# Silu in place, the weight sums of the last product one pair earlier, and other places for its first weights

## The chip, the cores and the metric

The kernel runs on one core of one Trainium2 chip. The metric is the device time of one execution in microseconds (us). A core has five engines that work side by side and wait for each other through semaphores: TensorE (PE, matrix products), VectorE (DVE), ScalarE (ACT), GpSimd (POOL) and SyncE (SP). Data moves between the main memory (DRAM) and the on-chip memory by DMA transfers; here SP, ACT and POOL issue them, each from its own queue of instructions, in order. An instruction whose condition is not met holds up all that stands behind it on the same engine.

## The reference

One layer of a hybrid encoder for 512 tokens of width 1024: four token mixers side by side, merged by gates; a cross-attention into 256 memory tokens; and a gated feed-forward part. The change lies in the feed-forward part alone:

```
hf = rms_norm(x, norm_ffn_pre)                     # 512 x 1024
u = dwconv_causal(hf @ w_up, ffn_dw) + ffn_dw_b    # 512 x 5632, three taps along the tokens
u_g, u_v = split(u, 2)                             # gate and value, 2816 columns each
yff = (silu(u_g) * u_v) @ w_down                   # 512 x 1024
x = x + rms_norm(yff, norm_ffn_post)
```

All of it is in float32.

## The kernel before

**Products.** A float32 operand is split into a high and a low part (ACT casts the high part, DVE subtracts it: tiles `wh` and `wl` for weights, `hth` and `htl` for activations), and each product is three matmuls: high by high, low by high, high by low. A matmul writes 512 columns of a bank of the accumulation memory (`ps_mm`, `ps_av`, `ps_sc`, `ps_tr`).

**The up product** has 22 blocks j of 128 columns, each with a gate half (i = 0) and a value half (i = 1). `done` takes a finished bank: ACT copies it into the tile `c` with bias and one tap, DVE adds the other two taps (L624), and behind the value half ACT computes Silu of the gate into a tile `th` of its own (L1681), and DVE multiplies it with the value into `qa` (L1683). There is one buffer for `th`. Nine of the blocks (j = 3, 5, ..., 19; the loop over q = 0 to 8) go through a scheme of seven products in place of eight, `seven(j)`. It loads the weights of the block into two tiles `wq`, forms sums of them on POOL, splits them in several steps, and its last split frees a tile `wq` for the next iteration. The block j + 1 follows in the plain way, mixed in.

**The last product** multiplies by `w_down`, 22 blocks of 128 rows taken as 11 pairs q = 0 to 10. It, too, goes by seven products in place of eight, so it needs sums of the four half blocks of a pair. The class `Sums` makes them during the up product. For each pair `load` brings two blocks of 512 KB into two tiles `wp` (L568, ACT's queue), `add` does four additions of 128x512 (L572 to L575), and `store` writes both tiles to a DRAM tensor `sums` (L579, ACT's queue). Pair 0 is added by DVE at the start of the loop; in iteration q, pair q + 1 is added by POOL; and pair 10 is loaded, added by DVE and stored behind the up product. The engine that adds matters for what stands behind it.

`down_jobs` then runs the last product in two phases over the pairs. In phase 0 a pair has two jobs of 12 matmuls each: job 0 needs half a block of `w_down` and one sum, job 1 two sums. SP loads the operands of a job into a tile `dw` (L591); ACT and DVE split it (L1652, L1653). POOL forms the sums on the side of the activations meanwhile (`pairs` and `qa`, L1664 to L1666 and L1870).

**Four places.** The tiles `wp`, `wq` and `dw` share four places of 512 KB, dw0 to dw3: `wp` takes turns in dw0 and dw1, `wq` in dw2 and dw3, and `dw` goes round all four. `dw_tile` keeps a counter for each name; without an entry the first tile goes to place 0:

```
i = ns.dw[name] = (ns.dw.get(name, -1) + 1) % n
return ns.fp.tile([P, D], dtype, tag=f"dw{first + i}", name=name)
```

A new tile in a place waits for the last user of the tile before.

**Order.** The order of the instructions on each engine is fixed when the kernel is built: a scheduler merges the jobs of the loops by its own estimates of time, and `issue_after` keeps a step behind a named instruction. Which of two steps stands first on an engine can therefore change with any edit.

Of the kernel before, what the change touches and what calls it, by code (L numbers as in the profile page):

```python
# [17 lines left out]
F32 = mybir.dt.float32  # L18
F32R = mybir.dt.float32r
AF = mybir.ActivationFunctionType  # L20
ALU = mybir.AluOpType
# [4 lines left out]
P = 128  # L26
S = 512
# [7 lines left out]
NF = DFF // P  # L35
# [51 lines left out]
def hybrid_layer(ctx: ExitStack, tc: tile.TileContext, a: dict, out: bass.AP):  # L87
    nc = tc.nc
    V, A, G, PE, SP = nc.vector, nc.scalar, nc.gpsimd, nc.tensor, nc.sync
# [1105 lines left out]
    ns = SimpleNamespace()  # L1195

    def then(f):

        return None, None, f
# [420 lines left out]
    def open_ffn():  # L1620
        bg.drain("n1")
        close(ns.work_)
        close(ns.xp_)
        close(ns.xm_)
        ns.fp_, ns.fp = new_pool("ffn", False)
        ns.work = ns.fp
        ns.quart = [ns.fp.tile([P, 4, S // 2], F32, tag=f"qa{q}", name="qa") for q in range(NF // 2)]
        ns.tok = [ns.fp.tile([P, 4, 4, S // 2], F32R, tag=n, name=n) for n in ("tokh", "tokl")]
        ns.post = ns.fp.tile([P, D], F32, name="g_ffn")
        ns.dw = {}  # L1630
        G.dma_start(ns.post, a["norm_ffn_post"][0].partition_broadcast(P))

    def dw_tile(name, n=4, first=0, dtype=F32):
# [34 lines left out]
    def up_jobs():  # L1668
        st, held = {}, []
        HALF = S // 2  # L1670
        first, second = slice(0, HALF), slice(HALF, S)

        def done(j, i, ps):
            if i == 0:
                st[j] = ns.fp.tile([P, 2, S], F32, tag="c", name="c", bufs=2)
            c, ch = st[j], i * NF + j
            st["first"] = A.activation(c[:, i], ps, AF.Identity, bias=pc("fb", ch), scale=pc("fdw2", ch)).ins
            st["taps"] = taps(c[:, i], ps, lambda k: pc("fdw01", k * 44 + ch), 3).ins
            if i == 1:
                th = ns.fp.tile([P, S], F32, tag="th", name="th")  # L1680
                A.activation(th, c[:, 0], AF.Silu)  # L1681
                x = ns.quart[j // 2][:, 2 * (j % 2):2 * (j % 2) + 2]
                V.tensor_tensor(x.rearrange("p a b -> p (a b)"), th, c[:, 1], ALU.mult)  # L1683

        def block(j, i):
            return cols(w_up, i * DFF + j * P)
# [1 line left out]
        def add_sums(q, eng, anchor):  # L1688
            with tc.issue_after(st[anchor]):
                ns.sums.add(q, eng)  # L1690

        def sums_step(what, q, anchor):
            if q < NF // 2:
                with tc.issue_after(st[anchor]):
                    getattr(ns.sums, what)(q)

        def plain(j, i, then=None):
            def body(hi, lo):
                ps = bank()
                channel_major(ps, (hi, lo), ns.hf)  # L1700
                done(j, i, ps)
                if then:
                    then()
            return *block(j, i), body
# [85 lines left out]
        for q, j in enumerate(range(3, NF - 2, 2)):  # L1790
            load_a, body_a, b, c, d, e = seven(j)
            if q:
                a = load_a, None, body_a
            else:
                a, early = (lambda: (ns,), None, lambda *w: body_first(*early)), []
                body_first = body_a
                yield then(lambda f=load_a: early.extend(f()))
                yield plain(2, 0)
                yield plain(2, 1, lambda: add_sums(0, V, "taps"))
            tail = {}  # L1800

            def first_half(hi, lo, tail=tail):
                tail.update(ps=bank(), w=(hi, lo))
                for k in range(4):
                    mm3(tail["ps"], hi[:, k], lo[:, k], ns.hf[0][:, k], ns.hf[1][:, k], k == 0, False)

            def second_half(j, tail=tail):
                hi, lo = tail["w"]
                for k in range(4, NK):
                    mm3(tail["ps"], hi[:, k], lo[:, k], ns.hf[0][:, k], ns.hf[1][:, k], False, k == NK - 1)  # L1810
                done(j, 1, tail["ps"])

            yield a
            yield plain(j + 1, 0)
            yield then(lambda q=q: sums_step("store", q, "first"))
            yield b
            yield (*block(j + 1, 1), first_half)
            yield then(lambda q=q: sums_step("load", q + 1, "taps"))
            if j + 4 > NF:
                ns.pair_sums = []  # L1820
                yield then(lambda: (down_places(("z7", 2)), down_sums(0, 1)))
            yield c
            yield d
            yield then(lambda j=j, f=second_half: f(j + 1))
            yield e
            yield then(lambda q=q: ns.sums.add(q + 1, G))
        q = NF // 2 - 1
        yield then(lambda: down_places(("tokh", 8), ("tokl", 1)))
        yield plain(NF - 1, 0, lambda: (sums_step("store", q - 1, "taps"), down_sums(2, 3)))
        yield plain(NF - 1, 1, lambda: (sums_step("load", q, "taps"), ns.sums.add(q), ns.sums.store(q),  # L1830
                                        down_sums(*range(4, NF // 2))))

    def down_jobs():
        pairs, hold, half = NF // 2, 4, S
# [229 lines left out]
```

## Time and profile before

| | |
|---|---|
| runs | 1078.36, 1080.32, 1084.20 us |
| median | 1080.32 us |
| profiled execution, its own time | 1078.18 us |
| its span | 1076.4 us (1.78 us lie around it) |
| mean granted TensorE clock | 0.987 |
| DMA moved | 169.42 MB, 157 GB/s |
| `wq` loads, `wp` loads, `wp` stores | 18, 22 and 22 of 512 KB |
| `dw` loads from `sums` | 44 of 256 KB |

The span is the stretch from the first to the last recorded instruction of the profiled execution, and all times of the trace count from its start. The mixers and the cross-attention take about the first 700 us, the up product runs to 936 us, the last product to about 1050 us, and the final normalisation to the end. Rows of the trace give the start, the length, the engine, the line of the kernel, and output and inputs; a bracket gives how long the engine had stood idle before, and what ended that. ACTq and SPq mark the instructions with which an engine issues a DMA. "x2" is two instructions in a row.

### The profile page before, as it was taken

How to read it: one execution, taken by the hardware profiler on the slowest of the kernel's cores; microseconds unless marked ns; L12 is line 12 of the kernel's file. 1: busy time of each engine (PE TensorE's matmuls, PEld its weight loads, DVE VectorE, ACT ScalarE, POOL GpSimd, SP SyncE). 2: the span in 40 equal slices, each digit the busy share in tenths (PEclk: the TensorE clock that was granted, in tenths of full speed). 3: DMA queues.
4: the chain of work that ended last, by engine and by line, in shares of the span. 5: the costliest groups of instructions: out<-in, count | busy, mean ns of one | idle time of the engine just before them, and what ended most of it. 6: DMA issues, size and time to landing. Idle time of an engine off the chain costs nothing.

```text
span 1076.4 us, 15302 instructions
## 1 busy us (share of the span) xinstructions
PE 1029.0 (96%) x5513; PEld 885.0 (82%) x5513; DVE 861.7 (80%) x1287; ACT 533.7 (50%) x898; POOL 317.3 (29%) x315
## 2 busy tenths in 40 slices
PE   9999999999999999999999999998999899767996
PEld 7888888888889888888888999996888888646885
DVE  7999998678787668878678987788776778876696
ACT  5322322386654566756345656545343553525662
POOL 3001000100111144232010421393665776891001
PEclk9999999999999999999999999999999999978999
DMA  8954333334534356766478332434566555446562
GB/s 272 302 156 103 98 98 98 93 89 119 151 111 126 87 145 190 192 179 178 147 226 270 131 119 78 124 112 156 176 197 201 191 181 172 156 157 235 183 211 85
DMA packets 194130, 169.42 MB, mean 157 GB/s; under 512 B 25295, under 2 KB 165692, under 8 KB 194053
## 3 DMA queue, kind: packets, MB, share of 16 engines
q1 hardware_dynamic: 185011, 136.69, 42.8%
q10 hardware_dynamic: 6482, 23.21, 5.8%
q0 software_dynamic: 2560, 8.54, 2.4%
q8 instruction: 43, 0.70, 0.3%
q14 instruction: 34, 0.28, 0.1%
HBM read 142.18 MB, written 26.23 MB: 156 GB/s over the span
## 4 chain that ended last, share of the span: by engine, by line
PE 70%; DVE 12%; DMA 8%; issue 4%; ACT 3%; POOL 2%; SPq 0%; ACTq 0%; DVEq 0%; POOLq 0%
PE ps_mm L244 33%; PE ps_av L244 18%; PE ps_tr L244 10%; PE ps_sc L244 6%; DVE wl L202 4%; DMA wq<-in_w_up 4%; DVE c L624 3%; DMA dw<-sums 2%; ACT wh L201 1%; PE ps_tr L250 1%; DVE qa L1683 1%; DMA ptl<-turned 1%; DMA turned<-e 1%; POOL pairs L1664 1%; DVE wl L1653 1%
## 5 line engine op out<-in xcount | busy, mean ns | idle before, releaser
L201 ACT CAST wh<-wr 128x1024 fp32r<-128x1024 f32 (+1 forms) x122 | 127.2, 1046 | 163.4 <-PE ps_mm L244 62.7
L202 DVE TENSOR_TENSOR wl<-wr,wh 128x1024 fp32r<-128x1024 f32 (+1 forms) x122 | 165.5, 1358 | 33.1 <-ACT wh L201 32.4
L244 PE MATMUL ps_mm<-hth,wl 128*128 128x512 f32 (+1 forms) x464 | 170.5, 376 | 1.2 <-DVE wl L202 1.2
L244 PE MATMUL ps_mm<-htl,wh 128*128 128x512 f32 (+1 forms) x464 | 170.5, 376 | 0.0
L244 PE MATMUL ps_mm<-hth,wh 128*128 128x512 f32 (+1 forms) x464 | 170.4, 376 | 0.0
L244 PEld LDWEIGHTS ps_mm<-hth,wl 128*128 128x128 f32 x464 | 85.5, 188 | 17.8 <-DVE wl L202 2.3
L244 PEld LDWEIGHTS ps_mm<-hth,wh 128*128 128x128 f32 x464 | 85.6, 188 | 14.8 <-ACT hth L164 0.3
L244 PEld LDWEIGHTS ps_mm<-htl,wh 128*128 128x128 f32 x464 | 85.5, 188 | 14.9
L244 PE MATMUL ps_av<-htl,wh 128*128 128x512 f32 (+1 forms) x256 | 94.6, 370 | 0.0
L244 PE MATMUL ps_av<-hth,wh 128*128 128x512 f32 (+1 forms) x256 | 94.6, 370 | 0.0
L244 PE MATMUL ps_av<-hth,wl 128*128 128x512 f32 (+1 forms) x256 | 94.5, 369 | 0.0
L697 DVE SCALAR_TENSOR_TENSOR y<-y,par,y 128x508 f32<-128x508 f32 (+29 forms) x120 | 83.1, 734 | 0.1
L1681 ACT ACTIVATE th<-c 128x512 f32<-128x512 f32 x22 | 13.9, 632 | 95.0 <-DVE qa L1683 57.0
L202 DVE TENSOR_TENSOR wl<-wq,wh 128x1024 fp32r<-128x1024 f32 (+1 forms) x27 | 37.4, 1385 | 26.2 <-ACT wh L201 26.2
L244 PEld LDWEIGHTS ps_av<-htl,wh 128*128 128x128 f32 x256 | 48.1, 188 | 8.0
L244 PEld LDWEIGHTS ps_av<-hth,wl 128*128 128x128 f32 x256 | 48.2, 188 | 7.8
L244 PEld LDWEIGHTS ps_av<-hth,wh 128*128 128x128 f32 x256 | 48.1, 188 | 7.5
L1653 DVE TENSOR_TENSOR wl<-dw,wh 128x1024 fp32r<-128x1024 f32 x32 | 42.5, 1330 | 13.4 <-ACT wh L1652 13.0
L244 PE MATMUL ps_tr<-hth,wh 128*128 128x512 f32 (+1 forms) x116 | 42.4, 366 | 8.7 <-ACT wh L201 8.7
L1652 ACT CAST wh<-dw 128x1024 fp32r<-128x1024 f32 x32 | 33.5, 1049 | 25.2 <-DMA dw<-sums 11.2
L244 PE MATMUL ps_tr<-hth,wl 128*128 128x512 f32 (+1 forms) x116 | 41.5, 358 | 0.9 <-DVE wl L202 0.9
L244 PE MATMUL ps_tr<-htl,wh 128*128 128x512 f32 (+1 forms) x116 | 41.7, 360 | 0.0
(556 smaller groups left out, 2826.2 us busy)
## 6 DMA issues: line engine op xcount, KB each, us to landing
wr<-in_w_in SPq DMA_DIRECT2D x38, 512.0 KB
wr<-in_w_gate SPq DMA_DIRECT2D x32, 512.0 KB
wr<-in_w_up SPq DMA_DIRECT2D x26, 512.0 KB
wp<-in_w_down ACTq DMA_DIRECT2D x22, 512.0 KB
sums<-wp ACTq DMA_DIRECT2D x22, 512.0 KB
dw<-sums SPq DMA_DIRECT2D x44, 256.0 KB
wq<-in_w_up SPq DMA_DIRECT2D x18, 512.0 KB
wr<-in_w_branch SPq DMA_DIRECT2D x16, 512.0 KB
```

The costliest lines, as they stand in the source:

```text
L201: last_weights[:] = [order(A.copy(hi, raw[:, :n])).ins, low.tensor_tensor(lo, raw[:, :n], hi.bitcast(F32), ALU.subtract).ins]
L202: low.tensor_tensor(lo, raw[:, :n], hi.bitcast(F32), ALU.subtract).ins]
L244: steps_of[:] = [PE.matmul(ps, lhs, rhs, start=start, stop=stop, skip_group_check=again).ins]
L250: turns.append(PE.transpose(ps, x, ident[:n, :n]).ins)
L624: ins = V.scalar_tensor_tensor(dst[:, s:], src[:, :S - s], w(k), dst[:, s:], ALU.mult, ALU.add)
L697: ins = V.scalar_tensor_tensor(dst[:, s:], src[:, :S - s], pc("conv_dw", k * 4 + j), dst[:, s:], ALU.mult, ALU.add)
L1652: A.copy(hi, x)
L1653: V.tensor_tensor(lo, x, hi.bitcast(F32), ALU.subtract)
L1664: G.tensor_tensor(t[:, 0], x[:, 1], x[:, 3], ALU.add)
L1681: A.activation(th, c[:, 0], AF.Silu)
L1683: V.tensor_tensor(x.rearrange("p a b -> p (a b)"), th, c[:, 1], ALU.mult)
```

## The change

Three things are changed. First, `ns.dw` starts with an entry: the first tile `dw` goes to place 2, so the last product begins in dw2 and dw3 and not in dw0 and dw1. Second, Silu writes over the gate half of `c`; the tile `th` is gone. Third, the sums go through the loop one pair earlier. Pair 0 is added and stored and pair 1 loaded ahead of the first iteration, DVE adds pair 1 in iteration 0, and in iteration q the pair q + 1 is stored, q + 2 loaded and, by POOL, added. Behind the loop only the store of pair 10 is left.

```diff
@@ open_ffn
-        ns.dw = {}
+        ns.dw = {"dw": 1}
@@ done, in up_jobs
             if i == 1:
-                th = ns.fp.tile([P, S], F32, tag="th", name="th")
-                A.activation(th, c[:, 0], AF.Silu)
+                A.activation(c[:, 0], c[:, 0], AF.Silu)
                 x = ns.quart[j // 2][:, 2 * (j % 2):2 * (j % 2) + 2]
-                V.tensor_tensor(x.rearrange("p a b -> p (a b)"), th, c[:, 1], ALU.mult)
+                V.tensor_tensor(x.rearrange("p a b -> p (a b)"), c[:, 0], c[:, 1], ALU.mult)
@@ ahead of the first iteration
-                yield plain(2, 0)
-                yield plain(2, 1, lambda: add_sums(0, V, "taps"))
+                yield plain(2, 0, lambda: (add_sums(0, V, "taps"), sums_step("store", 0, "taps")))
+                yield plain(2, 1, lambda: sums_step("load", 1, "taps"))
@@ the loop over q
-            yield then(lambda q=q: sums_step("store", q, "first"))
+            yield then(lambda q=q: (q or add_sums(1, V, "taps"), sums_step("store", q + 1, "first")) and None)
...
-            yield then(lambda q=q: sums_step("load", q + 1, "taps"))
+            yield then(lambda q=q: sums_step("load", q + 2, "taps"))
...
-            yield then(lambda q=q: ns.sums.add(q + 1, G))
-        q = NF // 2 - 1
+            yield then(lambda q=q: ns.sums.add(q + 2, G))
@@ behind the loop
-        yield plain(NF - 1, 0, lambda: (sums_step("store", q - 1, "taps"), down_sums(2, 3)))
-        yield plain(NF - 1, 1, lambda: (sums_step("load", q, "taps"), ns.sums.add(q), ns.sums.store(q),
-                                        down_sums(*range(4, NF // 2))))
+        yield plain(NF - 1, 0, lambda: (sums_step("store", NF // 2 - 1, "taps"), down_sums(2, 3)))
+        yield plain(NF - 1, 1, lambda: down_sums(*range(4, NF // 2)))
```

On SP, at the end of the up product, these loads begin the last product before the change. A number behind a name tells the tiles apart; dw_8922 is job 0 of pair 0, and dw_9000, dw_8928 and dw_9151 belong to the pairs 1 and 3, in dw2 and dw3.

```order
L591 DMA dw_9000<-sums_6869 128x512 [waits DMAHW4_49,DMAHW3_49,DVE_49]
L591 DMA dw_9000<-sums_6869 128x512 [waits DMAHW5_49,DMAHW4_49]
L591 DMA dw_8928<-in_w_down 128x512 [waits DMAHW7_49,DMAHW6_49,DVE_49]
L591 DMA dw_8928<-sums_6869 128x512 [waits DMAHW0_49]
L591 DMA dw_9151<-in_w_down 128x512 [waits DMAHW4_49,DMAHW7_49,DMAHW0_49,DVE_49]
L591 DMA dw_9151<-sums_6869 128x512 [waits DMAHW5_49]
L591 DMA dw_8922<-in_w_down 128x512 [waits DMASW5_49,DMAHW1_49,DMASW3_49,DMAHW3_49,PE_49,Pool_49]
L591 DMA dw_8922<-sums_6869 128x512
```

On SP at the same place after the change, dw_8916 and dw_8913 are the jobs 1 and 0 of pair 0, dw_9097 and dw_9039 those of pair 2, and dw_8919 and dw_8989 the jobs 0 and 1 of pair 1.

```order
L591 DMA dw_8916<-sums_6869 128x512 [waits DMAHW7_49,DMAHW3_49,DVE_49]
L591 DMA dw_8916<-sums_6869 128x512 [waits DMAHW0_49]
L591 DMA dw_8913<-in_w_down 128x512 [waits DMAHW3_49,DMAHW2_49,DVE_49]
L591 DMA dw_8913<-sums_6869 128x512 [waits DMAHW4_49]
L591 DMA dw_9097<-sums_6869 128x512 [waits DMAHW7_49,DMAHW0_49,DVE_49]
L591 DMA dw_9097<-sums_6869 128x512 [waits DMAHW1_49]
L591 DMA dw_9039<-in_w_down 128x512 [waits DMAHW3_49,DMAHW4_49,DMAHW2_49,DVE_49]
L591 DMA dw_9039<-sums_6869 128x512
L591 DMA dw_8919<-in_w_down 128x512 [waits DMASW5_49,DMAHW1_49,DMASW3_49,DMAHW5_49,PE_49,Pool_49]
L591 DMA dw_8919<-sums_6869 128x512 [waits DMAHW6_49]
L591 DMA dw_8989<-sums_6869 128x512 [waits DMAHW7_49,DMAHW4_49,PE_49]
L591 DMA dw_8989<-sums_6869 128x512 [waits DMAHW0_49]
```

The load that waits for POOL (the last addition of the pair that lies in dw0) is that of pair 0 before, and that of pair 1 now; both jobs of pair 0 and of pair 2 stand ahead of it.

On PE, the end of the 24 matmuls of pair 0 and the beginning of pair 1 after the change; `wr` and `hth` are split activations of pair 0 and pair 1, wh_8998 is the high part of dw_8916, wh_9042 that of dw_8919, wh_9105 that of dw_8989. Before, the first matmul behind the up product is the one on the high part of dw_8922.

```order
L244 MATMUL ps_av_9116<-wh_8998,wr_8922 128x512 [waits DVE_49,Activation_49]
L244 MATMUL ps_av_9116<-wl_8999,wr_8922 128x512
L244 MATMUL ps_av_9116<-wh_8998,wr_8923 128x512
L244 MATMUL ps_sc_9109<-wh_9042,hth_8992 128x512 [waits Activation_49]
L244 MATMUL ps_sc_9110<-wh_9042,hth_8992 128x512
L244 MATMUL ps_tr1_9111<-wh_9042,hth_8992 128x512
L244 MATMUL ps_tr0_9112<-wh_9042,hth_8992 128x512
L244 MATMUL ps_mm_9113<-wh_9105,hth_8992 128x512 [waits Activation_49]
L244 MATMUL ps_mm_9114<-wh_9105,hth_8992 128x512
L244 MATMUL ps_av_9115<-wh_9105,hth_8992 128x512
L244 MATMUL ps_av_9116<-wh_9105,hth_8992 128x512
L244 MATMUL ps_sc_9109<-wl_9043,hth_8992 128x512 [waits DVE_49]
```

Pair 0 stands in front of the wait for dw_8919, and pair 2 behind pair 1.

On DVE, ahead of the first iteration of the loop, before the change:

```order
L624 SCALAR_TENSOR_TENSOR c<-ps_av,par_398,c 128x511
L572 TENSOR_TENSOR wp<-wp 128x512
L202 TENSOR_TENSOR wl<-wq,wh 128x1024
L1653 TENSOR_TENSOR tokl<-qa,tokh 128x1024
L1683 TENSOR_TENSOR qa<-th,c 128x512
L573 TENSOR_TENSOR wp<-wp 128x512
L202 TENSOR_TENSOR wl<-wq,wh 128x512
L624 SCALAR_TENSOR_TENSOR c<-ps_mm,par_398,c 128x510
L574 TENSOR_TENSOR wp<-wp 128x512
L624 SCALAR_TENSOR_TENSOR c<-ps_mm,par_398,c 128x511
L575 TENSOR_TENSOR wp<-wp 128x512
L202 TENSOR_TENSOR wl<-wq,wh 128x1024
```

On DVE after the change, from the last tap that stands at the same place to the same split of `wq` at the end; the additions of pair 0 stand ahead of these rows.

```order
L624 SCALAR_TENSOR_TENSOR c<-ps_av,par_398,c 128x511
L1653 TENSOR_TENSOR tokl<-qa,tokh 128x1024
L1682 TENSOR_TENSOR qa<-c 128x512
L202 TENSOR_TENSOR wl<-wq,wh 128x512
L624 SCALAR_TENSOR_TENSOR c<-ps_mm,par_398,c 128x510
L624 SCALAR_TENSOR_TENSOR c<-ps_mm,par_398,c 128x511
L572 TENSOR_TENSOR wp<-wp 128x512
L573 TENSOR_TENSOR wp<-wp 128x512
L574 TENSOR_TENSOR wp<-wp 128x512
L575 TENSOR_TENSOR wp<-wp 128x512
L1774 TENSOR_TENSOR ps_tr_7103<-ps_tr_7103,mu 128x256
L202 TENSOR_TENSOR wl<-wq,wh 128x1024
```

The four additions here belong to pair 1, which has to be loaded first; the split of `wq` stands behind them. POOL's last addition of the pair in dw0 (L575) keeps its place behind 13 sums of activations; only the pair is another, 10 and not 9.

## The prediction

> **What bounds the kernel now.** I read the page first, for the engine that is busy most.
>
> ```profile
> PE 1029.0 (96%) x5513; PEld 885.0 (82%) x5513; DVE 861.7 (80%) x1287; ACT 533.7 (50%) x898; POOL 317.3 (29%) x315
> ```
>
> TensorE is busy for 96% of the span, so no edit can win more than TensorE's idle time and its slow clock. The windows view tells where those are. Its columns are the stretch and its length, the busy time and count of PE, PEld, DVE, ACT and POOL, the granted clock, the DMA share and GB/s.
>
> ```profile
> 930.00:940.00 10.00, 6.17 (x28) 4.77 (x26) 8.27 (x10) 4.35 (x7) 9.92 (x12) 0.99 0.29 105
> 940.00:950.00 10.00, 0.00 (x0) 0.00 (x0) 8.05 (x8) 3.73 (x8) 10.00 (x10) 0.50 0.24 72
> 950.00:960.00 10.00, 7.40 (x24) 5.96 (x25) 7.42 (x8) 4.01 (x5) 10.00 (x10) 0.66 0.66 214
> 960.00:970.00 10.00, 10.00 (x45) 8.20 (x44) 7.76 (x7) 2.32 (x3) 7.95 (x7) 1.00 0.45 162
> 970.00:980.00 10.00, 4.52 (x14) 3.29 (x13) 5.92 (x6) 4.59 (x7) 2.77 (x2) 0.70 0.87 302
> 980.00:1050.00 70.00, 70.00 (x309) 57.90 (x308) 55.64 (x61) 44.01 (x58) 2.56 (x4) 0.99 0.60 196
> 952.50:971.50 19.00, 18.70 (x72) 14.90 (x72) 14.29 (x13) 6.49 (x10) 15.45 (x14) 0.89 0.54 185
> ```
>
> PE does nothing for most of 936 to 952 and again around 971 to 977, and behind each pause the clock is down (0.66, 0.70). From 980 on it is full. The waits view, for the time behind 690 us, names what PE waited for (us in total, times, longest):
>
> ```profile
> PE ps_sc L244 <- ACT wh L1652: 21.9, 2, 16.4
> PE ps_tr L244 <- ACT wh L201: 8.7, 7, 1.6
> ```
>
> The first line is the two pauses, 16.4 and 5.5 us. The second is a short stall in seven of the nine iterations of the up product. The timeline of POOL, SP, ACT and PE gives the chain behind the first pause.
>
> ```profile
> 930.08 1.62 POOL L574 TENSOR_TENSOR wp<-wp 128x512 f32<-128x512 f32 x1
> 931.66 0.73 POOL L1664 TENSOR_TENSOR pairs<-qa 128x256 f32<-128x256 f32 x1
> ...
> 944.80 1.71 POOL L575 TENSOR_TENSOR wp<-wp 128x512 f32<-128x512 f32 x1
> 914.81 0.81 SPq L591 DMA_DIRECT2D dw<-sums  x2
> 919.50 0.33 SPq L591 DMA_DIRECT2D dw<-in_w_down  x1
> ...
> 946.54 0.33 SPq L591 DMA_DIRECT2D dw<-in_w_down  x1
> 946.92 4.78 SPq L591 DMA_DIRECT2D dw<-sums  x5
> 951.51 1.04 ACT L1652 CAST wh<-dw 128x1024 fp32r<-128x1024 f32 x1 [1.16 <-DMA dw<-sums]
> ...
> 955.01 1.04 ACT L1652 CAST wh<-dw 128x1024 fp32r<-128x1024 f32 x1 [1.94 <-DMA dw<-sums]
> 935.78 0.39 PE L244 MATMUL ps_av<-hth,wl 128*128 128x512 f32 x1
> 952.60 1.22 PE L244 MATMUL ps_sc<-wh,wr 128*128 128x512 f32 x2 [16.43 <-ACT wh L1652]
> ```
>
> POOL is through with three of four additions of pair 9 at 931.7, then does 13 sums of activations, and ends the fourth at 946.5. Only then may SP load pair 0 into dw0; ACT splits it at 951.5, and PE starts at 952.6. The pairs 1 and 3, in the other places, were loaded long before (914.8, 919.5). The second pause has the same form, with DVE in POOL's stead:
>
> ```profile
> 965.07 1.14 DVE L572 TENSOR_TENSOR wp<-wp 128x512 f32<-128x512 f32 x1
> ...
> 968.53 0.69 DVE L575 TENSOR_TENSOR wp<-wp 128x512 f32<-128x512 f32 x1
> 971.61 0.33 SPq L591 DMA_DIRECT2D dw<-in_w_down  x1
> 975.69 1.04 ACT L1652 CAST wh<-dw 128x1024 fp32r<-128x1024 f32 x1 [2.87 <-DMA dw<-sums]
> 976.78 1.22 PE L244 MATMUL ps_sc<-wh,htl 128*128 128x512 f32 x2 [5.48 <-ACT wh L1652]
> ...
> 980.36 0.58 PE L244 MATMUL ps_tr<-wl,htl 128*128 128x512 f32 x1
> ```
>
> Pair 10 lies in dw0 and dw1 in the middle of the last product; DVE adds it until 969.2, it is stored, and only then are those places loaded again (971.6).
>
> **Part 1, the start of the last product.** Both edits on the sums and on the places act here. The 24 matmuls of pair 0 now need dw2 and dw3 alone, whose loads at 914.8 and 919.5 are there before PE ends the up product at 936.2. At full clock a matmul takes 10 us / 44.1 = 0.227 us (309 in 70 us), so pair 0 is 24 x 0.227 = 5.4 us, all inside the old pause. The last three stand behind DVE's taps of the last up block and run a few us later; even if these were later than 952, they would cost 0.7 us.
>
> Then PE stands before pair 1, whose places are dw0 and dw1. POOL's order is unchanged, so job 0 comes as pair 0 did: split at 951.5, start at 952.6. This wait stays, and the pause is not 16.4 us shorter but only filled with 5.4 us. Four matmuls on, PE needs job 1, which comes with the second split of the old order, 955.0 + 1.04 = 956.1. From there 44 of the first 72 matmuls are left: 44 x 0.227 = 10.0 us, to 966.1. A slow clock may come on top. Before, the 72 took 971.3 - 952.6 = 18.7 us in place of 72 x 0.227 = 16.3, a loss of 2.4 us; with all of that again the end is 968.5, against 971.3.
>
> At that point PE went into the second pause. Its cause is gone: no sums lie in the places any more, pair 3 is loaded as soon as pair 1 is split (by 957), and a load takes about 4 us from 971.6 to 975.7, so it is there by 962. What is late next is the supply in general, and from 980 to 1050 that kept PE at 70.00 of 70. The next 12 matmuls then take 12 x 0.227 = 2.7 us and end between 968.8 and 971.2. Before, they ran from 976.78 to 981.5 (nine starts and the rest at 0.43 us in place of 0.227). The gain is 981.5 less 968.8 to 971.2, so **10.3 to 12.7 us**; I take 11.5. DVE's four additions of pair 10 (1.14 us the longest, in all about 4) go with it and free nothing else.
>
> [...]
>
> **Part 2, the start of the loop.** Here the change adds a wait. The rows of before, on DVE, ACT and POOL:
>
> ```profile
> 727.15 1.52 DVE L624 SCALAR_TENSOR_TENSOR c<-ps_mm,par,c 128x510 f32<-128x510 f32 x2
> ...
> 734.30 0.68 DVE L572 TENSOR_TENSOR wp<-wp 128x512 f32<-128x512 f32 x1
> ...
> 740.89 1.13 DVE L575 TENSOR_TENSOR wp<-wp 128x512 f32<-128x512 f32 x1
> 744.08 1.40 DVE L202 TENSOR_TENSOR wl<-wq,wh 128x1024 fp32r<-128x1024 f32 x1 [2.06 <-ACT wh L201]
> ...
> 747.00 1.97 DVE L202 TENSOR_TENSOR wl<-wr,wh 128x1024 fp32r<-128x1024 f32 x1 [0.85 <-ACT wh L201]
> 744.28 1.54 ACTq L568 DMA_DIRECT2D wp<-in_w_down  x2
> 750.10 1.29 POOL L572 TENSOR_TENSOR wp<-wp 128x512 f32<-128x512 f32 x1 [2.21 <-DMA wp<-in_w_down]
> ```
>
> Pair 0 is now added behind the taps of 727.15 and not from 734.30 on, some 6 us earlier; its last addition ends at about 735.7 in place of 742.0. Store and load of the next pair took 750.1 - 742.0 = 8.1 us from there to the first addition, so pair 1 is there at about 743.8. DVE comes to its additions at about 741, where the last tap stood before, and waits some 2.8 us. Four additions at 0.6 to 0.7 us, as in the row of 734.30, make it 746.2 to 746.6; beside POOL they took up to 1.14, which makes 748.4. Behind them stands the split of `wq` that started at 744.08, so it is 2.5 us late, or 4.7; and ACT's casts stand behind the trigger that waits for the store of pair 1. Of this 0.85 us goes into the idle time at 747.0. The bounds: nothing, if pair 1 is there by 741, since four additions then end by 743.4 and DVE waited until 744.08 anyway; and 5 us with slow additions and nothing absorbed. I take **2.5 us**, near the first row, and carry it to the end, since PE stalls in most of the iterations that follow.
>
> [...]
>
> **Part 3, Silu in place.** The waits view gives for DVE and for ACT:
>
> ```profile
> DVE qa L1683 <- ACT th L1681: 4.3, 5, 1.0
> ACT th L1681 <- DVE qa L1683: 57.0, 9, 7.7
> ```
>
> With one buffer, ACT may write `th` only when DVE has multiplied the block before; where two multiplications follow each other on DVE, the second waits up to 1.0 us for ACT. With Silu in `c`, which has two buffers, ACT can work ahead, and DVE's five waits (4.3 us) go. ACT's 57.0 us cost nothing by themselves; ACT is busy half of the time. DVE's next step there is the split that frees `wq`, and the reload of `wq` is what PE stalls for, 8.7 us in seven iterations. So the gain is between nothing, if another wait takes its place, and 4.3 us. I take **3 us**: PE stalls in seven of nine iterations, 1.2 us on average, and the waits that go are 0.9 us on average. A new wait could come from writing `c` in place, but a buffer of `c` was already free only after the multiplication.
>
> **The sum.** -11.5 + 2.5 - 3 = -12 us, with ends at -12.7 - 4.3 + 0 = -17 and -10.3 + 5 - 0 = -5.3. On the profiled execution's own time, 1078.18, this gives 1066.2 (1061 to 1073). The median of the runs is 2.1 above that execution, and on it the sum gives 1068.3. I forecast 1067.0 us, about 1.2% faster.
>
> **The rivals.**
>
> *The second pause moves.* Pair 1 waits for pair 10's store in dw1, and pair 3 for pair 1. If that store or those loads come 5 us later than the rows of before say, PE stands again at the head of pair 1 or pair 3 and the clock falls once more; the gain of Part 1 is then 11.5 - 5.5 = 6. For it: dw1 comes last in the new order, and the DMA share is 0.66 and 0.87 in those windows. Against it: five loads were issued in a row at 946.9, and the second split was there at 955.0. With the rest, -6 - 0.5: 1071 to 1076 us.
>
> *Nothing to be measured.* Pair 0 fills its 5.4 us, but no more is kept: Part 2 costs its 5 us, and Silu in place does nothing because the chain of `wq` finds another wait. 1077 to 1081 us. Against it stands that the second pause has no cause left.
>
> *Slower.* One mechanism: ACT's triggers. The load of a pair waits on ACT's queue for the store of the pair before, and what stands behind it waits too. In the row of 744.28 the trigger came 2 us behind the last addition. If, with the additions earlier and Silu no longer ahead, this wait comes to lie before the cast of `wh` that PE needs, it costs some 2.5 us in each of nine iterations, 22 us, and decides from about 1.6 us each (14.5 us against the gain of 11.5 + 3). Against it: the place of the triggers among the casts is the same in each iteration but the first. Its time is about 1086 to 1090 us.
>
> **How the numbers follow.** The forecast has 0.70, the moved pause 0.13, nothing measurable 0.10, slower 0.07. The forecast's own range, with the 2 us between the execution and the median, is 1061 to 1075. With the moved pause 0.83 is held, so the range goes from 1060 to 1078. A measurement of this kernel tells about 0.5% from no change, 5.4 us: faster is below 1074.9, slower above 1085.7. Faster is the forecast and half of the moved pause, 0.77; the other half and the third case give 0.16 for no change; slower 0.07.
>
> **What would show it.** Right: 24 matmuls between 936 and 946, a wait of PE for `wh` that ends near 952.6, one pause in place of two, and no `wp` row behind 950; no wait of DVE for Silu; and DVE waiting some 3 us for the load of pair 1 near 741. All times of the last product shift with what the loop has won or lost. Wrong: a pause of PE over 3 us behind 960, which is the first rival; stalls in the loop that are no shorter than 8.7 us in all, which takes the 3 us away; or a wait of PE over 3 us between 741 and 752, which makes Part 2 dearer.

## The result and the profile after

| | before | after |
|---|---|---|
| median of five runs | 1080.32 us (1078.36 to 1084.20) | 1072.24 us (1070.89 to 1074.34) |
| profiled execution, its own time | 1078.18 us | 1070.89 us |
| its span | 1076.4 us | 1069.1 us |
| mean granted TensorE clock | 0.987 | 0.986 |

The ratio of the times is 0.9922, with a 95% interval from 0.9894 to 0.995: the change makes the kernel 0.8% faster. The forecast was 1067.0 us in a range of 1060 to 1078; sign and range hold, and the gain is 8 us where the forecast has 13 (and its own sum 12).

The page of the kernel after says little. It has the same matmuls, and PE's busy time is even 3.7 us longer, since a matmul that runs at a lower clock counts as busy for longer (in the rows below one of 128x256 takes 0.28 us at 720.49, where the granted clock is 1.00, and 0.58 at 749.35, where it is 0.50).

```profile
PE 1032.7 (97%) x5513; PEld 887.5 (83%) x5513; DVE 865.4 (81%) x1287; ACT 538.2 (50%) x898; POOL 318.2 (30%) x315
```

So the time is followed through the program by landmarks on PE that both kernels have: the first matmul of the seven-product scheme in iteration 0 and in iteration 2, and the end of the up product, which the first matmul of the last product (942.42) follows at once in the kernel after. The timeline of PE of the kernel after gives them (start, length, engine and line, output and inputs):

```profile
720.49 0.28 PE L244 MATMUL ps_tr<-hth,wh 128*128 128x256 f32 x1
...
749.35 0.58 PE L244 MATMUL ps_tr<-hth,wh 128*128 128x256 f32 x1 [4.54 <-ACT wh L201]
752.24 0.58 PE L244 MATMUL ps_tr<-tokh,wh 128*128 128x256 f32 x1 [1.68 <-DVE ps_tr L1774]
775.50 0.34 PE L244 MATMUL ps_tr<-hth,wh 128*128 128x256 f32 x1
...
942.42 0.39 PE L244 MATMUL ps_sc<-wh,wr 128*128 128x512 f32 x1
...
951.94 0.77 PE L244 MATMUL ps_av<-wh,wr 128*128 128x512 f32 x1 [4.49 <-DVE c L624]
960.04 1.22 PE L244 MATMUL ps_sc<-wh,hth 128*128 128x512 f32 x2 [6.48 <-ACT wh L1652]
...
963.56 0.40 PE L244 MATMUL ps_sc<-wl,hth 128*128 128x512 f32 x1
```

The same two landmarks of the loop in the kernel before:

```profile
721.23 0.28 PE L244 MATMUL ps_tr<-hth,wh 128*128 128x256 f32 x1
...
768.64 0.38 PE L244 MATMUL ps_tr<-hth,wh 128*128 128x256 f32 x1 [0.81 <-ACT wh L201]
```

The up product ended there at 936.17 (the end of the row of 935.78 that the prediction shows), and TensorE stood until 952.60. The differences of these starts, and the rest up to the end of the span, are:

| stretch | before | after | difference |
|---|---|---|---|
| up to iteration 0 | 721.23 | 720.49 | -0.74 |
| iterations 0 and 1 | 47.41 | 55.01 | +7.60 |
| iteration 2 to the last product | 167.53 | 166.92 | -0.61 |
| last product to the end | 140.23 | 126.68 | -13.55 |
| span | 1076.4 | 1069.1 | -7.30 |

The change wins 13.6 us at its end and gives 7.6 back at the start of the loop. For the first two iterations, before and after, and for the rest of the loop after, the windows view has (columns as in the prediction):

```profile
721.23:768.64 47.41, 41.37 (x253) 35.94 (x252) 37.85 (x43) 20.49 (x31) 19.56 (x12) 1.00 0.51 167
```

```profile
720.49:775.50 55.01, 45.78 (x254) 40.16 (x252) 42.28 (x47) 21.40 (x31) 18.95 (x12) 0.88 0.56 185
775.50:942.42 166.92, 159.34 (x985) 141.13 (x985) 133.01 (x148) 80.90 (x115) 116.11 (x68) 1.00 0.58 186
```

Of the 7.6 us at the start, TensorE stands 3.2 us longer (9.2 in place of 6.0), and 4.4 us are the same matmuls at a slower clock (0.88). The windows view of the kernel after shows both places:

```profile
740.00:750.00 10.00, 5.16 (x33) 4.32 (x33) 3.39 (x4) 1.94 (x3) 2.90 (x3) 0.91 0.58 195
750.00:760.00 10.00, 8.32 (x40) 7.86 (x40) 9.97 (x12) 6.94 (x9) 3.06 (x3) 0.58 0.75 266
930.00:940.00 10.00, 10.00 (x52) 8.49 (x51) 9.47 (x10) 5.19 (x7) 6.03 (x4) 1.00 0.41 158
940.00:950.00 10.00, 7.46 (x33) 5.76 (x31) 9.86 (x13) 4.79 (x8) 10.00 (x12) 0.98 0.24 79
950.00:960.00 10.00, 1.62 (x3) 0.83 (x3) 7.25 (x7) 4.19 (x6) 10.00 (x10) 0.50 0.47 153
960.00:970.00 10.00, 9.96 (x37) 7.82 (x38) 8.35 (x7) 4.91 (x7) 10.00 (x9) 0.84 0.65 217
970.00:980.00 10.00, 10.00 (x46) 8.29 (x45) 10.00 (x8) 5.67 (x8) 10.00 (x8) 1.00 0.59 196
```

The waits view of the kernel after, behind 690 us, has the lines that stood at 21.9 and 8.7 us before (total, times, longest):

```profile
PE ps_tr L244 <- ACT wh L201: 12.1, 7, 4.5
PE ps_sc L244 <- ACT wh L1652: 6.5, 1, 6.5
```

In the last product one pause is left, 950 to 960, and it holds three matmuls of pair 0; the second, behind 970, is gone. In exchange PE now stands in the loop at 740 to 750, where before it was busy 9.15 of 10 us, and works at a clock of 0.58 behind it. The timelines of SP, ACT, DVE and POOL say what it stood for:

```profile
736.06 3.35 SPq L1744 DMA_DIRECT2D wq<-in_w_up  x2
...
734.88 0.33 ACTq L579 DMA_DIRECT2D sums<-wp  x1
737.25 0.34 ACTq L568 DMA_DIRECT2D wp<-in_w_down  x1
...
748.25 1.04 ACT L201 CAST wh<-wq 128x1024 fp32r<-128x1024 f32 x1 [6.76 <-DMA wq<-in_w_up]
...
747.05 0.69 DVE L572 TENSOR_TENSOR wp<-wp 128x512 f32<-128x512 f32 x1 [6.54 <-DMA wp<-in_w_down]
...
748.50 1.67 DVE L574 TENSOR_TENSOR wp<-wp 128x512 f32<-128x512 f32 x1
750.21 1.64 DVE L575 TENSOR_TENSOR wp<-wp 128x512 f32<-128x512 f32 x1
...
748.36 1.27 POOL L1737 TENSOR_TENSOR sums<-sums,wq 128x512 f32<-128x512 f32 x1 [2.42 <-DMA wq<-in_w_up]
749.59 1.71 POOL L1738 TENSOR_TENSOR wq<-wq 128x512 f32<-128x512 f32 x1
```

In the kernel before, the same reload of `wq` on SP and ACT:

```profile
736.19 3.30 SPq L1745 DMA_DIRECT2D wq<-in_w_up  x2
...
743.00 1.05 ACT L201 CAST wh<-wq 128x1024 fp32r<-128x1024 f32 x1 [1.29 <-DMA wq<-in_w_up]
```

Two things are late, not one. DVE waits 6.5 us for pair 1, as the prediction feared in a smaller size; PE's wait of 1.7 us at 752.24 hangs on the additions behind it. And the reload of `wq`, issued at the same time as before, takes 12.2 us in place of 6.8, so PE waits 4.5 us for its first cast.

### The profile page after: what moved, and what is told of

The parts are those of the page before. It is cut to its first block, busy times and chain, and to the rows that moved or that the text cites. A ratio compares the mean times of both kernels' runs of the same rounds, so it can differ in the third digit from the quotient of the medians.

```text
span 1069.1 us, 15300 instructions
## 1 busy us (share of the span) xinstructions
PE 1032.7 (97%) x5513; PEld 887.5 (83%) x5513; DVE 865.4 (81%) x1287; ACT 538.2 (50%) x898; POOL 318.2 (30%) x315
## 4 chain that ended last, share of the span: by engine, by line
PE 72%; DVE 10%; DMA 8%; issue 4%; ACT 3%; POOL 2%; SPq 0%; ACTq 0%; DVEq 0%; POOLq 0%
PE ps_mm L244 34%; PE ps_av L244 19%; PE ps_tr L244 10%; PE ps_sc L244 7%; DMA wq<-in_w_up 4%; DVE wl L202 4%; DVE c L624 3%; ACT wh L201 2%; DMA wp<-in_w_down 1%; PE ps_tr L250 1%; DMA dw<-sums 1%; DMA sums<-wp 1%; DVE qa L1682 1%; POOL pairs L1664 1%; DMA e<-in_w_in 1%
## 5 line engine op out<-in xcount | busy, mean ns | idle before, releaser
L244 PE MATMUL ps_tr<-hth,wh 128*128 128x512 f32 (+1 forms) x116 | 43.0, 371 | 12.1 <-ACT wh L201 12.1
L201 ACT CAST wh<-wq 128x1024 fp32r<-128x1024 f32 (+1 forms) x27 | 24.4, 904 | 54.0 <-PE ps_mm L244 26.6
```

The lines of the kernel that those rows point to most:

```text
L201: last_weights[:] = [order(A.copy(hi, raw[:, :n])).ins, low.tensor_tensor(lo, raw[:, :n], hi.bitcast(F32), ALU.subtract).ins]
L244: steps_of[:] = [PE.matmul(ps, lhs, rhs, start=start, stop=stop, skip_group_check=again).ins]
```

## The experiments

All kernels are the changed one with the edit shown, and all times are beside runs of the kernel before on the same chip. The stretches are those of the table above, each from one profiled execution; kernels with the same code at the start of the loop scatter there, four between 53.2 and 55.0 us and two others at 48.0 and 50.9. In the last product the changed kernel and those that alter only Silu or the start of the loop take 126.7 to 130.0, in part with a few instructions in another order. So differences below 3 us in these columns are not read by themselves.

**Silu back in a tile of its own.**

```diff
-                A.activation(c[:, 0], c[:, 0], AF.Silu)
+                th = ns.fp.tile([P, S], F32, tag="th", name="th")
+                A.activation(th, c[:, 0], AF.Silu)
...
-                V.tensor_tensor(x.rearrange("p a b -> p (a b)"), c[:, 0], c[:, 1], ALU.mult)
+                V.tensor_tensor(x.rearrange("p a b -> p (a b)"), th, c[:, 1], ALU.mult)
```

> The changed kernel with Silu written to a tile th of its own, as before. The prediction put Silu in place at 3 us, which gives 1075. Theory from the two profiles: six iterations in the middle of the loop took 22.38 us each before and 22.30 after, so it is worth 0.6 us at most, 1072 to 1073, with VectorE's waits for th back (about 4 us in 5 times) and hidden behind other waits of the chain.

Measured: 1073.22 us, ratio 0.9927 (0.9904 to 0.995), against 0.9922 for the change. The waits of DVE between 760 and 935 us, with `th` kept:

```profile
DVE ps_tr L1775 <- PE ps_tr L244: 12.3, 7, 2.8
DVE qa L1683 <- ACT th L1681: 4.5, 6, 0.8
```

and in the changed kernel, in the same window:

```profile
DVE ps_tr L1774 <- PE ps_tr L244: 15.1, 7, 3.8
```

PE's stalls for `wh` there come to 7.7 us with `th` and to 7.6 without. So Silu in place does take DVE's 4.5 us of waits away, as planned, but DVE then stands 2.8 us longer at its next step, which needs PE's result. The time gained ends there. The two ratios do not differ, as expected, but their intervals would hide some 4 us; what bounds the gain is DVE's waits.

**The new places alone, with the sums in their old order.** The loop, the lines ahead of it and the lines behind it are those of before; the entry in `ns.dw` and Silu in place stay.

```diff
-                yield plain(2, 0, lambda: (add_sums(0, V, "taps"), sums_step("store", 0, "taps")))
-                yield plain(2, 1, lambda: sums_step("load", 1, "taps"))
+                yield plain(2, 0)
+                yield plain(2, 1, lambda: add_sums(0, V, "taps"))
...
-            yield then(lambda q=q: (q or add_sums(1, V, "taps"), sums_step("store", q + 1, "first")) and None)
+            yield then(lambda q=q: sums_step("store", q, "first"))
```

> The sums stay in their old order (pair 0 by VectorE, pairs 1 to 9 by GpSimd in the loop, pair 10 inside the last product); the other two edits are made. Theory: the changed kernel's profile loses 7.6 us at the start of the loop to the earlier sums and wins 13.5 us behind the up product, of which filling the first pause with pair 0 is 5.4 us and the second pause with its slow clock the rest. Then this kernel has no loss at the start of the loop, wins 5.4 us and keeps the second pause: about 1080.3 - 5.4 - 0.6 = 1074 us. Rival: the places do nothing by themselves since pair 10 blocks dw0 and dw1 anyway, 1079 to 1081. Second rival: with the other places pair 10 no longer stands in the way either, and the full 13.5 come without the loss, 1066.

Measured: 1078.33 us, ratio 0.9979 (0.9967 to 0.9992): some 2 us, not the 6 expected. PE and DVE in its last product:

```profile
953.18 1.22 PE L244 MATMUL ps_sc<-wh,hth 128*128 128x512 f32 x2 [6.31 <-ACT wh L1652]
977.40 1.22 PE L244 MATMUL ps_sc<-wh,htl 128*128 128x512 f32 x2 [9.33 <-ACT wh L1652]
...
968.97 0.68 DVE L575 TENSOR_TENSOR wp<-wp 128x512 f32<-128x512 f32 x1
```

Pair 0 fills the first pause here too. But the second ends at 977.4, as before (976.8): pair 10 lies in the places until DVE has added it at 969.6 and it is stored, and PE, which comes earlier, waits longer, 9.3 us in place of 5.5.

**The sums alone, with the old places.**

```diff
-        ns.dw = {"dw": 1}
+        ns.dw = {}
```

> The changed kernel with the last product beginning in dw0 and dw1 as before. Theory: pair 0 waits for GpSimd's last addition again, so the first pause is its full 16 us and only the second pause goes: 1072.2 + 5.4 = 1077.6, up to 1079. Rival: the places are of no account because pair 1 waits at the same point in either case, 1072 to 1073.

Measured: 1074.39 us, ratio 0.9944 (0.9926 to 0.9962), less than the 1077.6 expected. PE has one pause, the first:

```profile
957.43 1.22 PE L244 MATMUL ps_sc<-wh,wr 128*128 128x512 f32 x2 [16.08 <-ACT wh L1652]
```

Together with the change and the kernel before this is a square of the last product (to the end of the span):

| | old places | new places |
|---|---|---|
| old sums | 140.2 | 139.7 |
| new sums | 130.8 | 126.7 |

The places are worth half a microsecond by themselves; the sums are worth 9.4 by themselves. Once the sums have moved, the places are worth 4.1 in this square, but the corner of 126.7 is the shortest of the kernels with both edits; with `th` kept it is 128.6, and with pair 0 added earlier (below) 130.0, which leaves 2.2 and 0.8. The ratios of the runs, 0.9944 and 0.9922, differ by 2.4 us, within their intervals. So the square shows that the places gain next to nothing while the second pause stands, and that the pause that goes is the larger part; what the places add after that is not measured well.

**The last addition of pair 10 by DVE.** What is left of the first pause should hang on POOL's last addition (row of 951.68 below), which stands behind 13 sums of activations. Here DVE does this one addition.

```diff
-            eng.tensor_tensor(b21, b21, b11, ALU.subtract)
+            (V if q == self.pairs - 1 else eng).tensor_tensor(b21, b21, b11, ALU.subtract)
```

> The changed kernel with one instruction moved: the fourth addition of pair 10 is done by VectorE in place of GpSimd, where it stood behind 13 sums of activations. Theory: this addition holds dw0 until 953 in the changed kernel's profile, and the pause of 6.5 us ahead of pair 1 hangs on it; it then ends near 940, pair 1 is there by 946, and the pause goes but for the 4.5 us for the taps: 1072.2 - 7 = 1065 us. Rival: pair 1 waits for something else (the activations of pair 1, split at 945 to 950, or the load of the other job), and the time stays within 1070 to 1073.

POOL and SP in the changed kernel:

```profile
951.68 1.27 POOL L575 TENSOR_TENSOR wp<-wp 128x512 f32<-128x512 f32 x1
...
952.98 0.33 SPq L591 DMA_DIRECT2D dw<-in_w_down  x1
```

DVE, PE and ACT with the edit:

```profile
939.12 1.21 DVE L575 TENSOR_TENSOR wp<-wp 128x512 f32<-128x512 f32 x1 [0.53 <-POOL wp L574]
...
948.65 0.63 PE L244 MATMUL ps_sc<-wh,hth 128*128 128x512 f32 x2
952.34 0.73 PE L244 MATMUL ps_sc<-wh,hth 128*128 128x512 f32 x2 [1.67 <-DVE hth L1653]
...
958.59 1.22 PE L244 MATMUL ps_sc<-wh,hth 128*128 128x512 f32 x2 [4.36 <-ACT wh L1652]
...
956.97 0.62 ACT L1652 CAST hth<-qa 128x512 fp32r<-128x512 f32 x1 [5.43 <-POOL qa L1666]
```

Measured: 1067.50 us, ratio 0.9875 (0.9849 to 0.9901). Pair 1 starts at 948.65, 11.4 us earlier than in the changed kernel, and the addition was what held it. Of that the last product keeps 4.0 us (122.7), and the 1065 expected is missed by 2.5: PE soon stands again, 1.7 and 4.4 us, the longer time because ACT's cast of the weights stands behind a cast that waits for POOL's sum of activations.

**Pair 1 added later in iteration 0.** The loss at the start of the loop has two candidates: DVE's wait ahead of the split of `wq`, and the transfers of pair 0 and 1 beside the reload of `wq`. This kernel takes the first away; the load of pair 1 stays where it is. The two new steps stand behind the steps `d` and `e` of iteration 0.

```diff
-            yield then(lambda q=q: (q or add_sums(1, V, "taps"), sums_step("store", q + 1, "first")) and None)
+            yield then(lambda q=q: q and sums_step("store", q + 1, "first") and None)
...
-            yield then(lambda q=q: sums_step("load", q + 2, "taps"))
+            if q:
+                yield then(lambda q=q: sums_step("load", q + 2, "taps"))
...
+            if not q:
+                yield then(lambda: (add_sums(1, V, "taps"), sums_step("store", 1, "taps")) and None)
...
+            if not q:
+                yield then(lambda: sums_step("load", 2, "taps"))
```

> The changed kernel with pair 1 still loaded ahead of the loop, but added by VectorE in the second half of iteration 0, so that VectorE doesn't wait for the load; its store and the load of pair 2 follow later. In the changed kernel and three variants of it the iterations 0 and 1 together take 53.1 to 55.0 us, against 47.4 before: 5.7 to 7.6 us lost. Theory: half of that is VectorE's wait of 4.6 to 6.5 us and the other half the late load of wq, which shares the DMA engines with the store of pair 0 and the load of pair 1. Then TensorE's first wait of 2.6 to 4.5 us for the split of wq stays and its second of 0.8 to 2.2 us goes: 50 to 51 us for the two iterations, 1069 to 1070 us in all. Rival: VectorE's wait is all of it, 47.5 us and 1066. Second rival: the wait only moves behind, no change.

**Pair 1 loaded later too**, right ahead of these additions, behind step d; the load ahead of the loop is left out. This takes the larger part of the second candidate away as well; the store of pair 0 stays. Beside the edit above:

```diff
-                yield plain(2, 1, lambda: sums_step("load", 1, "taps"))
+                yield plain(2, 1)
...
-                yield then(lambda: (add_sums(1, V, "taps"), sums_step("store", 1, "taps")) and None)
+                yield then(lambda: (sums_step("load", 1, "first"), add_sums(1, V, "taps"), sums_step("store", 1, "taps")) and None)
```

> The kernel pair1_added_later with the load of pair 1 issued some 10 us later, when the load of wq has landed. Theory: the late load of wq comes from sharing the DMA engines, so its split is back near 743 us on TensorE's clock of before, and the two iterations take 47.5 to 48.5 us: 1066 to 1067 us. Rival: the store of pair 0 alone holds up wq, or VectorE's adds do, and the two iterations stay at the value of pair1_added_later.

Measured: 1074.85 us, ratio 0.9963 (0.9948 to 0.9979) for the first, and 1073.39 us, 0.9944 (0.9912 to 0.9976) for the second.

| | iterations 0 and 1 | iteration 2 to the last product | last product |
|---|---|---|---|
| before | 47.4 | 167.5 | 140.2 |
| after | 55.0 | 166.9 | 126.7 |
| pair 1 added later | 50.5 | 173.2 | 128.6 |
| pair 1 loaded later too | 47.6 | 177.6 | 127.6 |

The first column does what the theory says. Without DVE's wait 2.7 to 4.5 us come back (53.2 to 55.0 less 50.5), and without the load of pair 1 another 3.0, which is the time of before. Each step has a second kernel further below: 50.7 with pair 1 added by POOL, and 46.8 with the load moved and one more edit that acts only near the end of the up product. The cast of `wh` shows the second step, first with pair 1 added later, then with it loaded later:

```profile
746.75 1.05 ACT L201 CAST wh<-wq 128x1024 fp32r<-128x1024 f32 x1 [5.52 <-DMA wq<-in_w_up]
```

```profile
744.59 1.05 ACT L201 CAST wh<-wq 128x1024 fp32r<-128x1024 f32 x1 [3.33 <-DMA wq<-in_w_up]
```

The reload of `wq` itself, from its issue on SP to the cast, gives the same order in all kernels of this document: 6.7 and 6.8 us with the old sums, 10.1 to 12.2 in the six kernels that store pair 0 and load pair 1 beside it, 8.0 and 8.7 in the two that only store pair 0, and 6.1 and 6.7 in the two that begin both earlier (below). So the transfers beside it are what delays it.

The second column took it all away again, which was not expected; both totals were forecast lower, at 1069 to 1070 and 1066 to 1067. ACT's waits between 760 and 935 us with pair 1 loaded later:

```profile
ACT wh L201 <- DMA sums<-wp: 15.6, 5, 10.0
```

and in the changed kernel:

```profile
ACT c L1680 <- DMA sums<-wp: 16.1, 5, 4.3
```

Here and there ACT waits some 16 us for stores, since the triggers of the next loads stand behind them. In the changed kernel Silu stands behind such a trigger, which hurts nobody; in the variant it is the cast of `wh`, which PE needs. So the step was moved to a worse neighbour in the iterations that follow. The windows view of that stretch, with pair 1 loaded later:

```profile
767.71:945.30 177.59, 165.48 (x987) 146.13 (x986) 129.77 (x149) 80.71 (x115) 115.37 (x71) 0.97 0.59 190
```

Of the 10.7 us more than in the changed kernel, TensorE stands 4.5 longer and is busy 6.1 longer at a clock of 0.97. That ACT's waits for stores are the cause is read from these traces; no kernel takes them away alone.

**Pair 1 added by POOL**, at the place where DVE adds it.

```diff
-            yield then(lambda q=q: (q or add_sums(1, V, "taps"), sums_step("store", q + 1, "first")) and None)
+            yield then(lambda q=q: (q or add_sums(1, G, "taps"), sums_step("store", q + 1, "first")) and None)
```

> The changed kernel with pair 1 added by GpSimd in place of VectorE; the order of GpSimd's sums changes in the loop and at the start of the last product too. Theory: VectorE's wait goes and the late load of wq stays, as in pair1_added_later, 50 to 51 us for the first two iterations; at the start of the last product GpSimd's order decides, so the total may lie on either side of 1070. Rival: GpSimd's additions hold up its sums of wq and the loss is larger than with VectorE, 55 us or more.

Measured: 1079.39 us, ratio 1.0008 (0.9993 to 1.0023). The start of the loop takes 50.7 us, like the kernel in which DVE adds later, but the rest of the up product takes 179.0. One window that covers the stretch, of this kernel:

```profile
770.00:951.00 181.00, 168.49 (x996) 149.93 (x996) 135.19 (x150) 82.75 (x116) 119.38 (x72) 0.96 0.57 183
```

and of the changed kernel:

```profile
770.00:951.00 181.00, 169.88 (x1042) 149.77 (x1040) 142.06 (x157) 86.06 (x123) 125.74 (x77) 1.00 0.56 181
```

PE is busy as long for 46 matmuls less, at a mean clock of 0.96: a good part of this loss is slow clock and not idle time. What lets the clock fall here stays open. ACT waits longer for `wq` in the loop (23.9 us against 15.6), but no stall of PE longer than 2.2 us is in the waits view of the loop behind iteration 1.

**Both: pair 1 loaded later and the last addition by DVE.** The edits are those shown for the one and the other.

> The edits of pair1_loaded_later and last_addition_by_dve together. If they are independent, 1072.2 - 5 - 4.7 = 1062 to 1063 us; if the later sums also make pair 10 late, 1065 to 1067.

Measured: 1070.00 us, ratio 0.9912 (0.9885 to 0.9939). Both expectations fail: the start takes 46.8 us and the last product 123.1, as meant, but the loop takes 177.8, with 19.4 us of ACT's waits for stores ahead of the cast of `wh`. The parts do not add up, and the loop has to keep its order.

**Pair 0 added earlier.** So the order of the loop is left as the change has it, and the chain is begun earlier instead: pair 0 is added and stored behind an earlier block, and the load of pair 1 is issued at 728.25 in place of 737.25.

```diff
+                        if (j, i) == (0, 0):
+                            add_sums(0, V, "taps")
+                            sums_step("store", 0, "taps")
+                        if (j, i) == (1, 0):
+                            sums_step("load", 1, "taps")
...
-                yield plain(2, 0, lambda: (add_sums(0, V, "taps"), sums_step("store", 0, "taps")))
-                yield plain(2, 1, lambda: sums_step("load", 1, "taps"))
+                yield plain(2, 0)
+                yield plain(2, 1)
```

> The changed kernel with pair 0 added, stored and pair 1 loaded some 8 to 10 us earlier still, among the split of the token sums; the pairs from 1 on keep their places in the loop. The two kernels that put pair 1 later won 3 and 6 us in the first two iterations and lost more in the later ones, where ScalarE waited for the stores and for GpSimd. Theory: the loss at the start is the load of wq and pair 1 at one time, and the later loss is the shift of the following pairs; then this kernel has the first two iterations at 47.5 to 49 us (53.1 to 55.0 in the changed kernel) and the rest of the loop as in the changed kernel, 1066 to 1068 us. Rival: the stretch ahead of the loop has no room on VectorE (9.67 of 10 us busy there before), and the four additions come out of TensorE's time there: 2 to 3 us back, 1069 to 1070.

**The same with the last addition by DVE**, by the edit of L575 shown above.

> pair0_added_earlier and last_addition_by_dve together. If the start of the loop and the start of the last product are independent, 1072.2 - 5 - 4.7 = 1062 to 1064 us; if what is won at the start is waited away at the start of the last product, 1066 to 1068.

Measured: 1069.07 us, ratio 0.9901 (0.9877 to 0.9924) for the first, and 1063.27 us, 0.9853 (0.9823 to 0.9882) for the second. ACT in the second:

```profile
744.01 1.05 ACT L201 CAST wh<-wq 128x1024 fp32r<-128x1024 f32 x1 [1.98 <-DMA wq<-in_w_up]
```

DVE waits for no load at 740.95 any more, the start takes 48.0 us, the rest of the loop 168.7 and the last product 124.6; the waits of PE behind 690 us name no pause over 3 us in the last product. This kernel is 16.8 us faster than the one before, and its interval ends where that of the change begins (0.9882 and 0.9894). With the old adder of pair 10 the start takes 50.9 us, and not the 47.5 to 49 expected; what is left there is DVE's additions of pair 1 ahead of the split (PE waits 2.5 us for `wl`). The two kernels have the same code there, so these 3 us are scatter. Its last product takes 130.0, 3.3 more than in the changed kernel, so most of the 4.1 us won at the start do not show in the total of the profiled execution; in the runs it is 1069.07, the number of the rival. The addition by DVE is worth 5.4 us of the last product here (130.0 to 124.6).

## Why the prediction was right, and where it was wrong

**The start of the last product: mechanism right, size within the scatter.** Predicted 11.5 us (10.3 to 12.7), measured 13.6 in the change, 11.6 with `th` kept and 10.2 with pair 0 added earlier, which have the same edits to the last product. Each step is in the rows. 21 matmuls of pair 0 run from 942.42, and three follow behind the last taps at 951.94. One pause remains; it ends at 960.04, which is 952.6 with the 6.3 us that the last product begins later, and 1.2 more. Nothing longer than 3 us stands behind it. What was not said is how the two parts depend on each other: the square above shows that the pause that goes is worth 9.4 us, and that filling the other is worth 0.5 as long as that one stands.

In the change the pause of 6.48 us costs more than its length: from 960.04 to 963.56 eight matmuls take 3.52 us in place of 8 x 0.227 = 1.82, 1.7 us more, and the row of 963.56 is the first that takes 0.40 us again. In the kernel before it took longer, 4.4 us behind the first pause (952.60 to 956.96) and 4.0 behind the second (976.78 to 980.78). With `th` kept pair 1 starts at 959.33, a second stop of 0.8 us follows, and the first matmul at full clock is that of 967.45, 8.1 us behind the start:

```profile
962.22 1.22 PE L244 MATMUL ps_mm<-wh,hth 128*128 128x512 f32 x2 [0.82 <-ACT wh L1652]
...
967.45 0.40 PE L244 MATMUL ps_sc<-wh,hth 128*128 128x512 f32 x1
```

With pair 0 added earlier it is 8.8 us, with a stop of 1.1. Behind 72 matmuls the changed kernel is 2.6 us ahead of the one with `th` kept, which is more than the 2.0 us by which their last products differ. So part of the 13.6 is luck with this stop.

**The start of the loop: this step failed.** The prediction put pair 1 "there at about 743.8", 8.1 us behind the last addition of pair 0, took 2.5 us, and bounded the cost by 5. The chain took 12.2 us (734.85 to 747.05): the trigger of the load came 2.4 us behind the last addition, much as before (2.3), but the load took 9.8 us in place of 5.8. The measured cost is 7.6 us, 5.8 to 6.4 in the three other kernels with the same start (53.2 to 53.8 less 47.4). Two things were left out of the sum. First, the transfers slow each other: the store of pair 0, the load of pair 1 and the reload of `wq` run together, and the reload, which the prediction left at its old 743, came at 748.25. The experiments put 3.0 us on the load of pair 1 and 2.7 to 4.5 on DVE's wait with the slow additions. Second, a pause of 4.5 us has its slow clock behind it (0.58 from 750 to 760), which the prediction reckoned for the last product and not here; slow matmuls make 4.4 of the 7.6 us. (A slip that changes no bound: with four additions of 1.14 us the split that started at 744.08 is 4.3 us late by the prediction's own rows, not 4.7.) Its own list said that a wait over 3 us between 741 and 752 would make this part dearer, and that is what happened.

The two traces show that the loads of SP and the store and load of ACT go over the same DMA engines. In the DMA view the packets of SP's queue alone, with the reload of `wq`, take 95.5% of the time of 16 engines from 737.6 to 738.6 before the change, and those of ACT's queue 99.5% from 735.5 to 737.5 after it; from 740 to 744 after it, with the reload and the load of pair 1 under way, SP's take 44.6% and ACT's 55.2%. The reload's 6.8 us become 12.2, and 3.0 us of the loop come back when the load of pair 1 is moved away. The value of 2.5 us holds none of this delay.

How the 3.0 and the 2.7 to 4.5 divide is read from two kernels whose later order differs as well; the start itself does not depend on that, but a scatter of up to 3 us does not let the division be sharper. The order of the reload's times does not rest on it.

**Silu in place: mis-sized.** Taken at 3 us, bounded by nothing and 4.3. From iteration 2 to the last product the change is 0.6 us shorter than before and 1.4 us shorter than with `th` kept (166.9 and 168.4), and the runs of the two kernels do not differ beyond their intervals. DVE's 4.5 us of waits went, but 2.8 of them came back at its next step, and PE's stalls for `wh` stayed (7.6 and 7.7 us). The prediction's own sign against this term came too: PE's stalls for `wh` in the loop are 12.1 us in all, with the wait of 4.5 among them, and not below 8.7. The bound below, "another wait takes its place", is nearest to what the runs show.

**The rivals.** The moved pause did not come. The slower case, ACT's triggers ahead of the cast of `wh`, did not come in the change either: ACT waits once like this, 4.05 us ahead of a cast at 737.63, and PE does not stop for it. But in the two kernels with pair 1 moved back such waits lie ahead of the cast (11.8 and 15.6 us in all), and the loop behind iteration 1 takes 6 to 11 us longer.

The sum was -11.5 + 2.5 - 3 = -12; by the stretches it is -13.6 + 7.6 - 0.6 - 0.7 = -7.3. The loop gave back what the prediction had taken for small. The -0.6 and -0.7 are below the scatter, and the 0.6 holds the other edits in that stretch as well.

## What to carry to other kernels

A step that is moved earlier brings its transfers along: look which loads are under way at the new place, and count the delay of those that the bottleneck needs, not only the wait of the step itself. When two pauses follow each other, ask of each what ends it by itself; filling the first was worth 0.5 us here while the second was pinned by another chain. And when a trigger that waits is moved, look at the instruction that stands right behind it in every later iteration.

## What was not expected of the hardware

An addition of 128x512 on DVE takes 0.69 us alone and 1.64 to 1.67 us while POOL adds beside it (rows of 747.05, 748.50 and 750.21, with POOL's rows of 748.36 and 749.59); in the kernel before, the longest was 1.14.

The windows view of 736 to 743, in the kernel after and then in the kernel before:

```profile
736.00:743.00 7.00, 6.69 (x46) 6.00 (x46) 4.47 (x6) 2.57 (x5) 0.00 (x0) 1.00 0.82 264
```

```profile
736.00:743.00 7.00, 7.00 (x46) 6.29 (x45) 6.02 (x9) 1.01 (x3) 1.38 (x1) 1.00 0.65 205
```

The 1 MB of `wq` took 6.8 us where the DMA share was 0.65, and 12.2 us where it was 0.82: the engines moved more, 264 GB/s in place of 205, and the one load that PE needed came 5.2 us later.
